# Masks of head pairs joined in one PSUM bank, and a retuned instruction order, in a two-layer hybrid attention decoder

## The chip, the cores and the metric

One core of a Trainium2 chip runs the whole program. Its engines are TensorE (PE, whose weight loads are listed as PEld), VectorE (DVE), ScalarE (ACT), GpSimd (POOL) and SyncE (SP), which issues the DMAs. The metric is the device time of one execution in microseconds (us), as the median of runs.

## The reference

Two layers on x of 512 tokens by 1024 channels. In a layer one normalised input goes through one input projection, whose columns are shared out among four groups of four heads of 64 channels each, and a gate. The outputs are normalised for each head, gated, projected and added to x. Cut to what the change touches:

```python
def fox_mixer(q, k, v, f_logit, fb):
    log_f = jax.nn.log_sigmoid(f_logit + fb)
    cum = jnp.cumsum(log_f, axis=1).transpose(0, 2, 1)
    for blk in range(T // Q_BLOCK):                       # 4 blocks of 128 queries
        s = q[:, :, t0:t1] @ k[:, :, :t1].T * ATTN_SCALE
        s = s + cum[:, :, t0:t1, None] - cum[:, :, None, :t1]
        mask = jnp.arange(t0, t1)[:, None] >= jnp.arange(t1)[None, :]
        p = _masked_softmax(s, mask)
        outs.append(p @ v[:, :, :t1])

def stick_breaking_mixer(q, k, v):
    for blk in range(T // Q_BLOCK):
        z = q[:, :, t0:t1] @ k[:, :, :t1].T * ATTN_SCALE
        mask = jnp.arange(t1)[None, :] < jnp.arange(t0, t1)[:, None]
        log_om = jnp.where(mask, jax.nn.log_sigmoid(-z), 0.0)
        suffix = lax.cumsum(log_om, axis=3, reverse=True) - log_om
        a = jnp.where(mask, jnp.exp(jax.nn.log_sigmoid(z) + suffix), 0.0)
        outs.append(a @ v[:, :, :t1])

for l in range(2):
    h = rmsnorm(x, norm_g[l])
    parts = split(h @ w_in[l])
    y = concat([hgrn2(...), fox_mixer(...), stick_breaking_mixer(...), nsa(...)])
    x = x + (headwise_rmsnorm(y) * out_norm_g[l] * silu(gate)) @ w_out[l]
return rmsnorm(x, final_norm_g)
```

HGRN2 is a gated linear recurrence in chunks of 64; NSA has a compressed, a selected and a window branch.

## The kernel before

The tokens lie in four blocks of 128. The input projection is done with split operands: the normalised and transposed x is held as a high part `hth` and a remainder `htl`, each weight as `whi` and `wlo`, and every product is three matmuls of 512 columns (hi by hi, hi by lo, lo by hi) for each of eight chunks, into PSUM tiles of the tag `pin`. ACT makes `whi`, DVE `wlo`, from the raw weights that SP's DMAs bring. PSUM has eight banks: four for `pin`, two for scores and for HGRN's small products (`pss`), one for attention outputs (`pso`), one for transposes of attention weights (`psm`).

FoX and stick-breaking go through the heads in pairs (i = 0, 1), through the four query blocks (`qb`, keys n = 128 to 512), and in a block through the two heads (s = 0, 1). A head's score takes a bank of `pss`: first a bf16 matmul of the identity with a 128x128 mask into the last 128 columns (in the trace `pss_pss<-one_c_bf`), then two score matmuls over all n columns. FoX then takes a negated maximum on DVE (`nm`) and an exponential on ACT with its row sum. Stick-breaking runs Abs, Exp, Ln on ACT, a DVE operation, a scan and a subtraction on DVE, and a last Exp on ACT, all on a tile `su` of the tag `t2`; the last of them that reads the scores is the subtraction. The function `turned` transposes the results with PE into the bank `psm` and copies them out as one tile `aT` (by `COPY`: DVE for FoX, ACT for the other two).

At the start each block of x is loaded (`XY`), its sum of squares is taken on ACT, `x_times_g` or `norm_t` multiplies it with the gain `gb` and the reciprocal root `xrs`, and PE transposes it. The multiply with the gain runs on POOL for the blocks in `POOLG`, else it is one DVE operation with the scaling:

```python
        if tb in POOLG:
            x_times_g(xg, gb, tb, 0, D, pool)
        norm_t(xg, xss, tb, None if tb in POOLG else gb)
```

The kernel isn't issued as it is written. All operations are recorded (so nearly all instructions have one line in the profile, that of the recorder), and `Program.order` then puts them in an order: it steps through a model of the five engines, and on each engine takes, of what could start, the operation with the lowest number in program order, shifted by `LEAD` (by tag) and `LAG` (projection matmuls go last). `RESERVE` keeps buffers of a tag back, `SLACK` stretches the model's costs and latencies, and `TIMES` sets when the pieces of each mixer come. `Program.issue` emits that order, and the engines follow their queues strictly. The figures in this model decide an order and nothing else.

Of the kernel before, what the change touches and what calls it, by code (L numbers as in the profile page):

```python
# [12 lines left out]
F32 = mybir.dt.float32  # L13
# [194 lines left out]
class Op:  # L208
    __slots__ = ("idx", "eng", "call", "reads", "writes", "cost", "deps", "new", "users", "wait", "prio", "lat",
                 "start", "done", "meth", "held", "pe", "form", "late")  # L210


class Program:
# [31 lines left out]
    def add(self, eng, call, writes, reads, cost, lat=0.0):  # L245
        o = Op()
        o.idx, o.eng, o.call, o.writes, o.reads, o.cost, o.lat = len(self.ops), eng, call, writes, reads, cost, lat
        o.prio, o.users, o.new, o.late = o.idx, [], [], False
# [24 lines left out]
        first = all(v.root.first is None for v in writes)  # L273
# [6 lines left out]
        o.late = eng == "pe" and first and writes[0].root.name in ("psf", "psb", "psq")  # L280
# [22 lines left out]
    def order(self):  # L303
# [34 lines left out]
        while n < len(ops):  # L338
            progress, nxt = False, math.inf
            for e in engines:  # L340
# [55 lines left out]
                elif e == "pe":  # L396
# [7 lines left out]
                    if o.late:  # L404

                        end = now + 0.08
                        begun = end
# [65 lines left out]
class Recorder:  # L473
# [28 lines left out]
    def cost(self, method, out, rest, kw, reads):  # L502
# [6 lines left out]
        elif self.name == "pe":  # L509
# [7 lines left out]
            load, stream, parts = m / 1.2, n / (2.227 if dt == F32R else 2.4), 1  # L517
# [36 lines left out]
def trunk(ctx: ExitStack, tc: tile.TileContext, cst, x, norm_g, w_in, lbl, fox_fb, pe_k, w1_k, w2_k,  # L554
# [234 lines left out]
    for l in range(nl):  # L789
# [387 lines left out]


        def fox(i):
            need(("fx", i))  # L1180
            Q1, Q2, K1, K2 = st["fx", i]
            for qb in range(NB):
# [32 lines left out]
        def stick(i):  # L1215
            need(("sb", i))
            Q1, K1, K2 = st["sb", i]
            for qb in range(NB):
# [3 lines left out]
                for s in range(2):  # L1222
                    ps = pss.tile([P, T], F32, name="psb", tag="pss")
                    pe.matmul(ps[:, qs], ident_b, mask_sb, start=True, stop=False, skip_group_check=True)
                    pe.matmul(ps[:, :n], Q1[:, s, qs], K1[:, s, :n], start=False, stop=False, skip_group_check=True)
                    pe.matmul(ps[:, :n], Q1[:, s, qs], K2[:, s, :n], start=False, stop=True, skip_group_check=True)
# [27 lines left out]
        def attend(qb):  # L1254
# [35 lines left out]
            for i in range(2):  # L1290
                us = {}
                for s in range(2):
                    for brs in ([slice(0, 2)] if qb < 2 else [slice(0, 1), slice(1, 2)]):
                        k = brs.stop - brs.start
                        ps = pss.tile([P, k, n], F32, name="psq", tag="pss")
                        pe.matmul(ps[:, :, qs], ident_b, mask_n.pattern([[0, k], [1, P]]), start=True, stop=False,
                                  skip_group_check=True)
# [153 lines left out]
TIMES = ((2.577, 1.29), (10.591, 0.535), (11.607, 0.725), (20.2, 0.497), (36.407, 0.974), (58.753, 0.361), (16.29, 1.112), (62.9, 0.953))  # L1451
RESERVE = {'gp_G': 1, 'pin_pin': 2, 'pso_pso': 3, 'sm_mr': 3, 't2_t2': 1, 'vp_vp': 3, 'psm_psm': 2}
# [39 lines left out]
```

## Time and profile before

| | |
|---|---|
| three runs | 672.25, 674.26, 674.77 us (median 674.26) |
| profiled execution, its own time | 672.69 us |
| its span | 670.9 us, mean granted clock 0.994 |
| PE busy | 655.9 us (98%), 5,387 matmuls |
| PEld busy | 515.1 us (77%) |
| DVE busy | 466.4 us (70%) |
| ACT busy | 419.0 us (62%) |
| POOL busy | 143.9 us (21%) |
| DMA moved | 63.68 MB, mean 95 GB/s |

The span runs from the first to the last instruction on the chip; the 1.8 us between it and the execution's time lie around it. Matmuls are pipelined, so the records of two of them overlap, and the distance of their starts tells what each takes of the engine. A time in brackets at the end of a row of the timeline is how long the engine stood idle before it, and the name behind it is what ended that.

### The profile page before, as it was taken

The page shows a single profiled execution, that of the slowest core. Times are in us where ns is not written, and L with a number is a line of the kernel's source. Part 1 is how long each engine was busy: PE and PEld are TensorE (multiplying, and loading weights), DVE is VectorE, ACT ScalarE, POOL GpSimd, SP SyncE. Part 2 cuts the span into 40 slices and gives each one's busy share as a digit, 9 for nine tenths or more (in the row PEclk, how much of TensorE's full clock was granted, in tenths as well). Part 3 has the DMA queues.
Part 4 walks back from the last instruction along what each step waited for, and adds up shares of the span by engine and source line. Part 5 has one row for each costly group of instructions (what it writes and reads, how often), then busy time and mean ns, then how long its engine had stood idle before and what let it go on. Part 6 is the DMA issues. An engine that isn't in the chain of part 4 may idle for free.

```text
span 670.9 us, 13843 instructions
## 1 busy us (share of the span) xinstructions
PE 655.9 (98%) x5387; PEld 515.1 (77%) x5387; DVE 466.4 (70%) x990; ACT 419.0 (62%) x942; POOL 143.9 (21%) x173
## 2 busy tenths in 40 slices
PE   7999999999999999999999999999999999999996
PEld 4788977778877777777888898777788777777774
DVE  4745588765878969754672476976678988786543
ACT  5455455666777879765353654566586778887632
POOL 3100223412333312210100030450223232122010
PEclk8999999999999999999999999999999999999998
DMA  6544243460433104112352425337124321420112
GB/s 235 164 105 113 67 136 98 113 156 1 127 94 97 48 32 143 64 64 94 104 161 59 106 64 144 83 95 190 33 71 133 90 63 41 127 79 5 44 64 94
DMA packets 67162, 63.68 MB, mean 95 GB/s; under 512 B 20484, under 2 KB 51736, under 8 KB 67096
## 3 DMA queue, kind: packets, MB, share of 16 engines
q1 hardware_dynamic: 67096, 62.80, 32.9%
q8 instruction: 42, 0.69, 0.4%
q14 instruction: 24, 0.20, 0.1%
HBM read 52.79 MB, written 4.19 MB: 85 GB/s over the span
## 4 chain that ended last, share of the span: by engine, by line
PE 93%; DVE 2%; issue 1%; DMA 1%; ACT 1%; SPq 1%; POOL 0%; POOLq 0%
PE pin_pin L490 64%; PE pss_pss L490 13%; PE pso_pso L490 9%; PE psm_psm L490 7%; DMA one_XY<-in_x 1%; SPq L490 1%; ACT t_t L490 0%; DMA sm_w<-in_nsa_cmp_w_v 0%; DVE wp_wlo L490 0%; ACT wp_whi L490 0%; POOL sm_rs L490 0%; DVE sm_vcm L490 0%; DVE one_htl L490 0%; DVE one_XY L490 0%; DVE sm_ng L490 0%
## 5 line engine op out<-in xcount | busy, mean ns | idle before, releaser
L490 PE MATMUL pin_pin<-wp_whi,one_hth 128*128 128x512 f32 (+1 forms) x384 | 152.7, 399 | 1.8 <-ACT wp_whi L490 1.8
L490 PE MATMUL pin_pin<-wp_wlo,one_hth 128*128 128x512 f32 (+1 forms) x384 | 152.8, 398 | 0.2 <-DVE wp_wlo L490 0.2
L490 PE MATMUL pin_pin<-wp_whi,one_htl 128*128 128x512 f32 (+1 forms) x384 | 150.1, 393 | 0.0
L490 DVE TENSOR_TENSOR wp_wlo<-wp_raw,wp_whi 128x1024 fp32r<-128x1024 f32 (+1 forms) x80 | 96.4, 1210 | 52.9 <-ACT wp_whi L490 52.2
L490 PE MATMUL pin_pin<-one_hth,wp_wlo 128*128 128x512 f32 x256 | 103.6, 405 | 0.0
L490 PE MATMUL pin_pin<-one_htl,wp_whi 128*128 128x512 f32 x256 | 103.0, 402 | 0.0
L490 PE MATMUL pin_pin<-one_hth,wp_whi 128*128 128x512 f32 x256 | 102.5, 401 | 0.0
L490 ACT ACTIVATE wp_whi<-wp_raw 128x1024 fp32r<-128x1024 f32 (+1 forms) x80 | 83.4, 1043 | 27.2 <-PE pin_pin L490 20.1
L490 POOL TENSOR_TENSOR sm_rs<-sm_ssv,one_mhalf 128x2 f32<-128x2 f32 (+1 forms) x48 | 41.4, 863 | 199.0 <-DVE sm_ssv L490 161.0
L490 PEld LDWEIGHTS pin_pin<-wp_whi,one_hth 128*128 128x128 f32 x384 | 72.4, 189 | 15.2 <-ACT wp_whi L490 2.0
L490 PEld LDWEIGHTS pin_pin<-wp_wlo,one_hth 128*128 128x128 f32 x384 | 72.6, 189 | 11.9 <-DVE wp_wlo L490 0.9
L490 PEld LDWEIGHTS pin_pin<-wp_whi,one_htl 128*128 128x128 f32 x384 | 72.5, 189 | 11.7
L490 ACT ACTIVATE t_t<-pss_pss,sm_nm 128x128 f32<-128x128 f32 (+3 forms) x96 | 50.9, 543 | 29.3 <-DVE sm_nm L490 25.6
L490 PE MATMUL pss_pss<-qk_qk,qk_qk 128*128 128x512 f32 (+3 forms) x224 | 66.8, 378 | 0.0
L490 DVE TENSOR_REDUCE sm_nm<-pss_pss 128x1 f32<-128x384 f32 (+5 forms) x80 | 43.2, 549 | 23.9 <-PE pss_pss L490 13.3
L490 PEld LDWEIGHTS pin_pin<-one_htl,wp_whi 128*128 128x128 f32 x256 | 48.3, 189 | 10.9 <-issue 0.4
L490 PEld LDWEIGHTS pin_pin<-one_hth,wp_wlo 128*128 128x128 f32 x256 | 48.3, 189 | 10.8 <-issue 0.7
L490 PE MATMUL psm_psm<-one_c_ident,t_t 128*128 128x128 f32 x320 | 55.6, 276 | 0.8 <-DVE sm_vcm L490 0.8
L490 PEld LDWEIGHTS pin_pin<-one_hth,wp_whi 128*128 128x128 f32 x256 | 48.2, 188 | 9.6 <-issue 0.4
L490 ACT ACTIVATE pa_pa<-pa_pa 128x512 f32<-128x512 f32 (+4 forms) x90 | 51.0, 568 | 6.8 <-DVE pa_pa L490 5.6
L490 POOL TENSOR_TENSOR h_h<-h_h,h_h 128x512 f32<-128x512 f32 (+1 forms) x16 | 26.5, 1658 | 118.4 <-ACT h_h L490 112.5
L490 PEld LDWEIGHTS psm_psm<-one_c_ident,t_t 128*128 128x128 f32 x320 | 39.7, 142 | 14.7 <-issue 3.2
(183 smaller groups left out, 1062.8 us busy)
## 6 DMA issues: line engine op xcount, KB each, us to landing
wp_raw<-in_w_in SPq DMA_DIRECT2D x56, 256.0 KB, 3.4
wp_raw<-in_w_in SPq DMA_DIRECT2D x28, 512.0 KB, 4.1
wp_raw<-in_w_out SPq DMA_DIRECT2D x16, 512.0 KB, 3.6
qk_qk<-qk_qk SPq DMA_DIRECT2D x16, 256.0 KB, 3.2
one_XY<-in_x SPq DMA_DIRECT2D x4, 512.0 KB, 7.7
pa_pa<-in_x SPq DMA_DIRECT2D x8, 256.0 KB, 3.2
xres<-one_XY SPq DMA_DIRECT2D x8, 256.0 KB, 2.0
pa_pa<-xres SPq DMA_DIRECT2D x8, 256.0 KB, 3.6
```

What stands on the lines that cost most here:

```text
L490: fn(*[r(a) for a in args], **{k: r(v) for k, v in kw.items()})
```

## The change

For the first two query blocks FoX and stick-breaking compute both heads of a pair in one bank: `heads_of(qb)` gives ((0, 1),) for qb below 2 and ((0,), (1,)) otherwise. One mask matmul covers both (`masked`, 2 x 128 columns). Stick-breaking runs each elementwise operation once over both heads, but for the scan, which stays one for each head, and has one `turned` for both. FoX takes the two maxima in one reduction; its exponentials stay one for each head. NSA's scores use the same helper and stay as they are.

In the model that sets the order, the load of bf16 weights costs m/4.8 in place of m/1.2, and the special case for the first matmul into a score bank (`late`) is gone. Several numbers of the tables change, `POOLG` and `LATEG` among them: block 2 in place of block 3 has its gain multiplied on POOL at the start, and at the boundary of the layers block 0 has its gain multiplied ahead of its root.

```diff
-        o.late = eng == "pe" and first and writes[0].root.name in ("psf", "psb", "psq")
...
-                    if o.late:
-
-                        end = now + 0.08
-                        begun = end
...
-            load, stream, parts = m / 1.2, n / (2.227 if dt == F32R else 2.4), 1
+            load, stream, parts = m / (4.8 if dt == BF else 1.2), n / (2.227 if dt == F32R else 2.4), 1
...
+        def heads_of(qb):
+
+            return ((0, 1),) if qb < 2 else ((0,), (1,))
+
+        def masked(name, mask, k, n, qs):
+
+            ps = pss.tile([P, k, n], F32, name=name, tag="pss")
+            pe.matmul(ps[:, :, qs], ident_b, mask.pattern([[0, k], [1, P]]), start=True, stop=False, skip_group_check=True)
+            return ps
...
-                for s in range(2):
-                    ps = pss.tile([P, T], F32, name="psf", tag="pss")
-                    pe.matmul(ps[:, qs], ident_b, mask_n, start=True, stop=False, skip_group_check=True)
-                    pe.matmul(ps[:, :n], Q1[:, s, qs], K1[:, s, :n], start=False, stop=False, skip_group_check=True)
-                    pe.matmul(ps[:, :n], Q2[:, s, qs], K2[:, s, :n], start=False, stop=True, skip_group_check=True)
-                    us += softmax(ps[:, None, :n], den[:, s:s + 1])
+                for hs in heads_of(qb):
+                    ps = masked("psf", mask_n, len(hs), n, qs)
+                    for j, s in enumerate(hs):
+                        pe.matmul(ps[:, j], Q1[:, s, qs], K1[:, s, :n], start=False, stop=False, skip_group_check=True)
+                        pe.matmul(ps[:, j], Q2[:, s, qs], K2[:, s, :n], start=False, stop=True, skip_group_check=True)
+                    us += softmax(ps, den[:, hs[0]:hs[-1] + 1])
...
-                    u = t2.tile([P, T], F32, name="su", tag="t2")[:, :n]
-                    act.activation(u, ps[:, :n], AF.Abs)
+                    u = t2.tile([P, k, n], F32, name="su", tag="t2")
+                    act.activation(u, ps, AF.Abs)
                     act.activation(u, u, AF.Exp, scale=-1.0)
                     act.activation(u, u, AF.Ln, bias=1.0)
-                    dve.scalar_tensor_tensor(u, ps[:, :n], 0.0, u, op0=OP.min, op1=OP.subtract)
-
-                    dve.tensor_tensor_scan(u.flip(), ones.to_broadcast([P, n]), u.flip(), 0.0, op0=OP.mult, op1=OP.add)
-                    dve.tensor_tensor(u, u, ps[:, :n], OP.subtract)
+                    dve.scalar_tensor_tensor(u, ps, 0.0, u, op0=OP.min, op1=OP.subtract)
+
+                    for j in range(k):
+                        dve.tensor_tensor_scan(u[:, j].flip(), ones.to_broadcast([P, n]), u[:, j].flip(), 0.0, op0=OP.mult, op1=OP.add)
+                    dve.tensor_tensor(u, u, ps, OP.subtract)
                     act.activation(u, u, AF.Exp)
-                    aT[s] = turned([u[:, kb * P:(kb + 1) * P] for kb in range(qb + 1)], COPY[1])
+                    t = turned([u[:, j, kb * P:(kb + 1) * P] for j in range(k) for kb in range(qb + 1)], COPY[1])
...
-POOLG = (3,)
-LATEG = (0, 1, 2, 3)
-SLACK = (1.15, 0.1, 1.0)
+POOLG = (2,)
+LATEG = (1, 2, 3)
+SLACK = (1.129, 0.119, 1.12)
```

Four of the eight pairs in `TIMES` change as well, `RESERVE` loses `pso_pso` and gains `wp_whi`, and `LEAD` changes for `qk_qk` (60 to 100) and `wp_wlo` (300 to 290).

PE's order at the first FoX block of the first layer, before (`one_c_bf` holds the bf16 identity and mask, `qk_qk` queries and keys, `pss_pss_0` and `pss_pss_1` are the two score banks):

```order
L490 MATMUL pin_pin_3_125<-one_hth_0_68,wp_wlo_0_99 128x512
L490 LDWEIGHTS one_c_bf_0_127
L490 MATMUL pss_pss_1_96<-one_c_bf_0_127 128x128
L490 MATMUL pss_pss_1_96<-qk_qk_1_137,qk_qk_0_136 128x128
L490 MATMUL pss_pss_1_96<-qk_qk_3_139,qk_qk_2_138 128x128
L490 LDWEIGHTS one_c_bf_0_127
L490 MATMUL pss_pss_0_95<-one_c_bf_0_127 128x128
L490 MATMUL pss_pss_0_95<-qk_qk_1_137,qk_qk_0_136 128x128
L490 MATMUL pss_pss_0_95<-qk_qk_3_139,qk_qk_2_138 128x128
L490 MATMUL pin_pin_3_125<-one_hth_0_68,wp_whi_0_104 128x512
```

The same place after the change:

```order
L484 MATMUL pin_pin_3_125<-one_hth_0_68,wp_wlo_0_99 128x512
L484 LDWEIGHTS one_c_bf_0_127
L484 MATMUL pss_pss_0_95<-one_c_bf_0_127 128x256
L484 MATMUL pss_pss_0_95<-qk_qk_1_137,qk_qk_0_136 128x128
L484 MATMUL pss_pss_0_95<-qk_qk_3_139,qk_qk_2_138 128x128
L484 MATMUL pss_pss_0_95<-qk_qk_1_137,qk_qk_0_136 128x128
L484 MATMUL pss_pss_0_95<-qk_qk_3_139,qk_qk_2_138 128x128
L484 MATMUL pin_pin_3_125<-one_hth_0_68,wp_whi_0_104 128x512
```

One mask of 256 columns stands where two of 128 stood, in one bank in place of two, and the four score matmuls follow it unchanged.

POOL's order at the start, before (`sm_xrs_0` to `sm_xrs_3` are the reciprocal roots of the four blocks, `one_XY` is x, `h4_h4_0` the gain; `h4_h4_3` and `h4_h4_4` are the normalised blocks 2 and 3):

```order
L490 TENSOR_TENSOR sm_xrs_0_91<-sm_xrs_0_91,one_mhalf_0_73 128x1
L490 TENSOR_TENSOR sm_xrs_1_92<-sm_xrs_1_92,one_mhalf_0_73 128x1
L490 TENSOR_TENSOR sm_xrs_2_93<-sm_xrs_2_93,one_mhalf_0_73 128x1
L490 TENSOR_TENSOR sm_xrs_3_94<-sm_xrs_3_94,one_mhalf_0_73 128x1
L490 TENSOR_TENSOR h4_h4_4_79<-one_XY_0_67,h4_h4_0_75 128x1024
```

and after:

```order
L484 TENSOR_TENSOR sm_xrs_0_91<-sm_xrs_0_91,one_mhalf_0_73 128x1
L484 TENSOR_TENSOR sm_xrs_1_92<-sm_xrs_1_92,one_mhalf_0_73 128x1
L484 TENSOR_TENSOR h4_h4_3_78<-one_XY_0_67,h4_h4_0_75 128x1024
L484 TENSOR_TENSOR sm_xrs_2_93<-sm_xrs_2_93,one_mhalf_0_73 128x1
L484 TENSOR_TENSOR sm_xrs_3_94<-sm_xrs_3_94,one_mhalf_0_73 128x1
```

POOL's large multiply moved from behind all four roots to between the second and the third, and is block 2's now. In the same place DVE multiplies block 3 with gain and root, and scales block 2 by its root alone.

DVE's order around the copies of the compressed values (`sm_vcm`, of which PE's next transposes need the bank `psm_psm_0`), before:

```order
L490 TENSOR_TENSOR pa_pa_0_110<-pa_pa_0_110,one_c_ropec_0_128 64x32
L490 COPY sm_vcm_0_172<-psm_psm_0_71 32x64
L490 TENSOR_TENSOR sm_kcs_0_170<-sm_kcs_0_170,pa_pa_0_110 64x32
L490 TENSOR_TENSOR one_XY_0_67<-pso_pso_0_156,sm_rs_1_164 128x128
L490 COPY sm_vcm_0_172<-psm_psm_0_71 32x64 x2
L490 SCALAR_TENSOR_TENSOR sm_ng_0_130<-sm_ng_0_130,pa_pa_4_114 128x48
L490 TENSOR_TENSOR sm_K1c_0_171<-sm_kcs_0_170,sm_K1c_0_171 64x32
L490 COPY sm_vcm_0_172<-psm_psm_0_71 32x64
```

and after:

```order
L484 STREAM_SHUFFLE pa_pa_0_110<-sm_kcr_0_169 64x32
L484 TENSOR_TENSOR pa_pa_0_110<-pa_pa_0_110,one_c_ropec_0_128 64x32
L484 TENSOR_TENSOR sm_kcs_0_170<-sm_kcs_0_170,pa_pa_0_110 64x32
L484 COPY sm_vcm_0_172<-psm_psm_0_71 32x64 x3
L484 TENSOR_TENSOR sm_K1c_0_171<-sm_kcs_0_170,sm_K1c_0_171 64x32
L484 COPY sm_vcm_0_172<-psm_psm_0_71 32x64
L484 SCALAR_TENSOR_TENSOR sm_ng_0_130<-sm_ng_0_130,pa_pa_4_114 128x48
```

Three of the four copies stand together now, a 64x32 subtraction stands ahead of the fourth, and the normalisation of `one_XY` and the operation on `sm_ng` have left the places between them. On PE, eight products into `pso_pso` (64x128) and one score of 384 columns stand now between the matmuls that these copies read and the next transposes, where eight projection matmuls stood.

## Rows read from the trace of the kernel before

**Rows 1.** Busy time of PE, PEld, DVE, ACT, POOL in one stretch, clock, DMA.

```profile
25.00:330.00 305.00, 302.94 (x2588) 239.23 (x2588) 214.03 (x466) 195.40 (x449) 67.07 (x79) 1.00 0.34 93
```

**Rows 2.** Waits of PE over the span: total us, times, longest.

```profile
PE pss_pss L490 <- issue: 3.0, 4, 1.3
...
PE psm_psm L490 <- DVE sm_vcm L490: 0.8, 2, 0.5
```

**Rows 3.** Timeline of PE, a 256-wide head under a 128-wide mask: start, duration.

```profile
132.74 0.23 PE L490 MATMUL pss_pss<-one_c_bf 128*128 128x128 bf16 x1
...
133.10 0.40 PE L490 MATMUL pin_pin<-wp_wlo,one_hth 128*128 128x512 f32 x1
```

**Rows 4.** Timeline of PE, 256-wide scores under a 256-wide mask.

```profile
244.44 0.28 PE L490 MATMUL pss_pss<-one_c_bf 128*128 128x256 bf16 x1
...
244.80 0.40 PE L490 MATMUL pin_pin<-wp_whi,one_hth 128*128 128x512 f32 x1
245.03 0.40 PE L490 MATMUL pin_pin<-wp_wlo,one_hth 128*128 128x512 f32 x1
```

**Rows 5.** Timeline of PE, two 128-wide heads next to each other.

```profile
112.12 0.23 PE L490 MATMUL pss_pss<-one_c_bf 128*128 128x128 bf16 x1
...
112.99 0.40 PE L490 MATMUL pin_pin<-one_htl,wp_whi 128*128 128x512 f32 x1
```

**Rows 6.** Timeline of PE, a 128-wide head by itself.

```profile
154.44 0.23 PE L490 MATMUL pss_pss<-one_c_bf 128*128 128x128 bf16 x1
...
155.02 0.78 PE L490 MATMUL pso_pso<-vp_vp,gp_G 128*128 128x64 f32 x6
```

**Rows 7.** Timeline of all engines in the opening norm.

```profile
11.73 2.44 DVE L490 TENSOR_TENSOR wp_wlo<-wp_raw,wp_whi 128x1024 fp32r<-128x1024 f32 x2
...
13.11 1.06 ACT L490 ACTIVATE t_t<-one_XY 128x1024 bf16<-128x1024 f32 x1 [0.20 <-DMA one_XY<-in_x]
...
15.24 0.40 PE L490 MATMUL pin_pin<-wp_wlo,one_hth 128*128 128x512 f32 x1
...
15.39 0.74 DVE L490 SCALAR_TENSOR_TENSOR h_h<-one_XY,sm_xrs,h_h 128x512 f32<-128x512 f32 x1
...
16.84 3.56 DVE L490 SCALAR_TENSOR_TENSOR h_h<-one_XY,sm_xrs,h_h 128x512 f32<-128x512 f32 x2 [0.59 <-POOL sm_xrs L490]
...
17.28 2.57 POOL L490 TENSOR_TENSOR h_h<-one_XY,h_h 128x1024 f32<-128x1024 f32 x1
...
17.35 0.60 PE L490 MATMUL pss_pss<-one_c_ident,h_h 128*128 128x128 f32 x4
...
19.30 0.60 PE L490 MATMUL pss_pss<-one_c_ident,h_h 128*128 128x128 f32 x4
...
21.06 0.66 PE L490 MATMUL pss_pss<-one_c_ident,h_h 128*128 128x128 f32 x4 [0.69 <-DVE one_htl L490]
...
22.85 0.50 PE L490 MATMUL pin_pin<-wp_wlo,one_hth 128*128 128x512 f32 x1 [0.22 <-DVE wp_wlo L490]
```

**Rows 8.** Page and PE's timeline: a burst, its wait, the instruction queue.

```profile
PE 655.9 (98%) x5387; PEld 515.1 (77%) x5387; DVE 466.4 (70%) x990; ACT 419.0 (62%) x942; POOL 143.9 (21%) x173
...
q8 instruction: 42, 0.69, 0.4%
...
114.83 1.21 PE L490 MATMUL pss_pss<-h_h 64*16 64x16 f32 x127
117.12 0.17 PE L490 MATMUL pss_pss<-h_h 64*16 64x16 f32 x1 [1.09 <-issue]
```

**Rows 9.** Timeline around the copies of compressed values.

```profile
219.08 0.23 DVE L490 COPY sm_vcm<-psm_psm 32x64 f32<-32x64 f32 x1
...
219.37 0.33 PE L490 MATMUL psm_psm<-one_c_ident,t_t 128*128 128x128 f32 x1 [0.52 <-DVE sm_vcm L490]
```

**Rows 10.** Groups on t_t: min, median, max ns, and forms.

```profile
L490 ACT ACTIVATE t_t<-t_t x96: 292/471/641, 161.6 to 569.3; 128x128 f32<-128x128 f32 x24, 128x256 f32<-128x256 f32 x24, 128x384 f32<-128x384 f32 x24, 128x512 f32<-128x512 f32 x24
...
L490 DVE TENSOR_TENSOR_SCAN t_t<-one_ones,t_t x32: 409/811/1224, 163.1 to 565.6; 128x128 f32<-128x128 f32 x8, 128x256 f32<-128x256 f32 x8, 128x384 f32<-128x384 f32 x8, 128x512 f32<-128x512 f32 x8
```

More of the change, by code (lines that the diff above doesn't have):

```diff
@@ L209 @@
     __slots__ = ("idx", "eng", "call", "reads", "writes", "cost", "deps", "new", "users", "wait", "prio", "lat",
-                 "start", "done", "meth", "held", "pe", "form", "late")
+                 "start", "done", "meth", "held", "pe", "form")
 class Program:
@@ L247, in add @@
         o.idx, o.eng, o.call, o.writes, o.reads, o.cost, o.lat = len(self.ops), eng, call, writes, reads, cost, lat
-        o.prio, o.users, o.new, o.late = o.idx, [], [], False
+        o.prio, o.users, o.new = o.idx, [], []
         if eng == "pe" and writes[0].root.tag.name == "pin_pin":
@@ L272, in add @@
                 r.acc = keep
-        first = all(v.root.first is None for v in writes)
         if eng == "pe":
@@ L1221, in stick @@
                 qs = slice(qb * P, n)
[L1222 to L1226, printed above, removed]
-                    u = t2.tile([P, T], F32, name="su", tag="t2")[:, :n]
-                    act.activation(u, ps[:, :n], AF.Abs)
+                for hs in heads_of(qb):
+                    k = len(hs)
+                    ps = masked("psb", mask_sb, k, n, qs)
+                    for j, s in enumerate(hs):
+                        pe.matmul(ps[:, j], Q1[:, s, qs], K1[:, s, :n], start=False, stop=False, skip_group_check=True)
+                        pe.matmul(ps[:, j], Q1[:, s, qs], K2[:, s, :n], start=False, stop=True, skip_group_check=True)
+                    u = t2.tile([P, k, n], F32, name="su", tag="t2")
+                    act.activation(u, ps, AF.Abs)
                     act.activation(u, u, AF.Exp, scale=-1.0)
                     act.activation(u, u, AF.Ln, bias=1.0)
-                    dve.scalar_tensor_tensor(u, ps[:, :n], 0.0, u, op0=OP.min, op1=OP.subtract)
-                    dve.tensor_tensor_scan(u.flip(), ones.to_broadcast([P, n]), u.flip(), 0.0, op0=OP.mult, op1=OP.add)
-                    dve.tensor_tensor(u, u, ps[:, :n], OP.subtract)
+                    dve.scalar_tensor_tensor(u, ps, 0.0, u, op0=OP.min, op1=OP.subtract)
+                    for j in range(k):
+                        dve.tensor_tensor_scan(u[:, j].flip(), ones.to_broadcast([P, n]), u[:, j].flip(), 0.0, op0=OP.mult, op1=OP.add)
+                    dve.tensor_tensor(u, u, ps, OP.subtract)
                     act.activation(u, u, AF.Exp)
-                    aT[s] = turned([u[:, kb * P:(kb + 1) * P] for kb in range(qb + 1)], COPY[1])
+                    t = turned([u[:, j, kb * P:(kb + 1) * P] for j in range(k) for kb in range(qb + 1)], COPY[1])
+                    for j, s in enumerate(hs):
+                        aT[s] = t[:, j * (qb + 1):(j + 1) * (qb + 1)]
                     yield
@@ L1294, in attend @@
                         k = brs.stop - brs.start
-                        ps = pss.tile([P, k, n], F32, name="psq", tag="pss")
-                        pe.matmul(ps[:, :, qs], ident_b, mask_n.pattern([[0, k], [1, P]]), start=True, stop=False,
-                                  skip_group_check=True)
+                        ps = masked("psq", mask_n, k, n, qs)
                         pe.matmul(ps, Q1[i][:, s, qs], K1[:, brs, :n], start=False, stop=False, skip_group_check=True)
@@ L1448, in trunk @@
     pr.issue(ctx, tc, order)
-TIMES = ((2.577, 1.29), (10.591, 0.535), (11.607, 0.725), (20.2, 0.497), (36.407, 0.974), (58.753, 0.361), (16.29, 1.112), (62.9, 0.953))
-RESERVE = {'gp_G': 1, 'pin_pin': 2, 'pso_pso': 3, 'sm_mr': 3, 't2_t2': 1, 'vp_vp': 3, 'psm_psm': 2}
+TIMES = ((2.577, 1.29), (10.591, 0.713), (11.607, 0.725), (20.2, 0.497), (50.852, 0.974), (58.753, 0.235), (13.999, 1.112), (62.9, 0.953))
+RESERVE = {'gp_G': 1, 'pin_pin': 2, 'sm_mr': 3, 't2_t2': 1, 'vp_vp': 3, 'psm_psm': 2, 'wp_whi': 2}
 FILL = (0, 1, 2, 6, 3, 4, 5, 7)
-LEAD = {'pin_pin': 20, 'psm_psm': -20, 'pss_pss': 10, 'qk_qk': 60, 'sm_mr': -80, 't2_k1': 120, 'vp_vp': -180, 'wp_wlo': 300, 'pa_junk': 0, 't2_t2': 0, 't2_oT': 40, 'gp_G': 10, 'pa_pa': 10, 'sm_nm': -10, 'one_htl': 100, 'one_hth': -20, 'wp_whi': 20}
+LEAD = {'pin_pin': 20, 'psm_psm': -20, 'pss_pss': 10, 'qk_qk': 100, 'sm_mr': -80, 't2_k1': 120, 'vp_vp': -180, 'wp_wlo': 290, 'pa_junk': 0, 't2_t2': 0, 't2_oT': 40, 'gp_G': 10, 'pa_pa': 10, 'sm_nm': -10, 'one_htl': 100, 'one_hth': -20, 'wp_whi': 20}
 FULL = (128, 128)
```

## The prediction

> **What bounds the kernel now.** The busy times by stretch come first [rows 1]: in the 305 us from 25 to 330 TensorE (PE) is busy for 302.94, VectorE (DVE) for 214.03, ScalarE (ACT) for 195.40, GpSimd (POOL) for 67.07, and the granted clock is full. So only two things can shorten the kernel: less work on PE, or fewer waits of PE. PE's waits were read next [rows 2]: the whole span has 3.0 us at "issue" (four times, waiting for nothing that the profile shows), and 0.8 us for the DVE copies into `vcm`; what else is listed lies in the first 25 us. Nearly all the rest is work. From there I went to PE's timeline, where the masks, the start and the two kinds of waits are priced. Work saved on ACT and DVE is worth nothing by itself; it counts only through what PE waits for. The last projection and the normalisation behind it keep their order, so I cost the tail at nothing.
>
> **What a removed mask is worth.** Sixteen of 32 masks of the first two query blocks go (2 layers x 2 pairs x 2 kinds of attention x 2 blocks = 16 joint blocks), and the 16 that stay are 256 columns wide. The 64 score matmuls of these blocks stay as they are. PE's records overlap, so I price by starts. A 256-wide head with a 128-wide mask occupies 132.74 to 133.10, 0.36 us [rows 3]. The same two score matmuls under a 256-wide mask, which the NSA scores have already, take 244.44 to 244.80, again 0.36 [rows 4]. So a mask twice as wide costs no more here; in this stream something other than its columns sets the pace.
>
> - Second query block (n = 256): now two heads at 0.36 are 0.72. Joint, it is 0.36 for mask and first head plus two 256-wide matmuls. A 512-wide matmul follows the one before it after 0.233 (244.80 to 245.03) [rows 4], and I take half of that for each, 2 x 0.117 = 0.23. Together 0.59, 0.13 saved, four times a layer.
> - First query block (n = 128): a lone head takes 154.44 to 155.02 with the projection matmul behind it, so 0.58 - 0.233 = 0.35 [rows 6]. Two adjacent heads take 112.12 to 112.99 less 0.233, 0.64, or 0.106 a matmul [rows 5]. Joint: 0.35 + 2 x 0.106 = 0.56. Three of four blocks of a layer have their heads apart in the order of before (0.70, saving 0.14), one has them adjacent (saving 0.08).
>
> A layer saves 4 x 0.13 + 3 x 0.14 + 0.08 = 1.02, both **2.0 us**. The bounds: 0 if the masks' columns were what PE is paced by (then nothing is removed, only rearranged), and 16 x 0.14 = 2.2 if all were apart.
>
> The Trainium skill, "TensorE: Matmul & The Clock Gate", section "Back-to-back issue gap", gives for the spacing of isolated warm matmuls the columns over 2.4 GHz plus 2.5 ns, and warns that short ones under-count this way. By that formula 16 masks of 256 columns instead of 32 of 128 would save an estimated 16 x 2.5 ns = 0.04 us: nothing. The two equal 0.36 us speak against it, and its own warning agrees with them.
>
> **The longer chains.** A joint block hands the transposes both heads at once, so the first head's comes later. For stick-breaking at n = 256 the chain is four passes of ACT, two of DVE and two scans. The longest passes, of 512 columns, take 0.641 on ACT [rows 10] and one of DVE's 0.74 (at 15.39) [rows 7]; a scan over 256 columns takes no more than the median of 0.811 [rows 10]: 4 x 0.64 + 2 x 0.74 + 2 x 0.81 = 5.7 us at work, perhaps 8 with the work that stands between in the queues (a factor I choose: DVE and ACT are busy two thirds of the time [rows 1]). What hides it is the distance in PE's order. Between the last score of such a block and its first transpose stand at least 37 matmuls of 512 columns, 37 x 0.233 = 8.6 us, beside 17 or more others; for n = 128, at least 25, 5.8 us, for a chain of some 4. The joint FoX blocks have at least 9, 2.1 us, for a maximum and two exponentials (about 1.2). So I take no wait. If the cover is gone, PE waits for the rest of the chain, and behind the transposes on PE's queue stands the projection that feeds everything else.
>
> **The start.** Here DVE waits for POOL. The two multiplies of DVE at 16.84 take 3.56 us, where a single one takes 0.74 at 15.39, and beside them POOL multiplies two SBUF operands from 17.28 for 2.57 [rows 7]. So DVE's second multiply stands still until POOL is done. PE then waits 0.69 at 21.06 and 0.22 at 22.85: 0.9 us. With POOL's multiply moved to block 2 and ahead of the reciprocal roots of blocks 2 and 3, it can begin when block 2 of x is in (ACT starts on it at 13.11) and DVE's pair of subtractions (11.73 to 14.17) ends. So I place it at 14.2 to 16.8. Then it holds up the multiply that ran at 15.39 until 16.8; that ends at 17.5, and PE's transposes of it stood at 17.35: up to 0.2 of wait. On POOL the roots of blocks 2 and 3 follow, so DVE's scaling of block 2 ends at perhaps 18.5, and PE wants that only at 19.30. Sum: -0.9 + 0.2 = -0.7, of which I take **-0.6**. Bounds: -0.9 if POOL hides entirely; and +0.6 if POOL gets its operands first and the second of the two subtractions waits for it, 2.57 late, to 16.7: PE needs that weight at 15.24, a wait of 1.5 in place of 0.9.
>
> The Trainium skill, "SBUF — State Buffer", section "Who interferes with whom", has this as a rule: POOL shares a port pair with DVE, a DVE instruction with two SBUF inputs is held by a POOL instruction that reads, and whoever issues first blocks the other for its whole length. The 3.56 us agree with it, and by it the bad bound is the likelier the earlier block 2 lands.
>
> **The waits at issue.** All four lie within bursts of tiny HGRN matmuls, as the 127 in 1.21 us with a wait of 1.09 behind them [rows 8]. PE's matmuls and weight loads are 5,387 each, 10,774 instructions, and the instruction queue moved 42 packets [rows 8], about 256 instructions each; 127 matmuls with their loads are 254, one packet. I read them as PE running out of fetched instructions when a burst uses up packets faster than they come. The change shifts where packets begin: 16 matmuls fewer and other neighbours of the bursts. By the new order's counts two of the four would shrink: **-0.5**, between -2 and +1.
>
> **The single bank of transposes.** PE waits 0.52 at 219.37 because its next transposes need the bank that the DVE copy of 219.08 empties, the fourth of four [rows 9]; 0.8 in both layers [rows 2]. In the new order only eight short products and one score stand between the matmuls and the next transposes, where 8 projection matmuls stood (8 x 0.233 = 1.9 us), and DVE still has a small subtraction ahead of the fourth copy. Against that, the copies come earlier in DVE's queue. Eight products and a score are about 0.9 us of cover, less by 1.0; the copies come perhaps 0.3 to 0.6 sooner. So the wait of 0.4 a layer grows to about 0.75: **+0.7** for both. Bounds -0.8 (none) and +2.5.
>
> The other retuned numbers move instructions elsewhere, where PE waits for nothing now; I cost them at nothing. The cover is the distance between an operand and its use on PE, and a row that lost it would cost one pass, up to 0.6 us.
>
> **Sum.** -2.0 - 0.6 - 0.5 + 0.7 = -2.4. The profiled execution took 672.69, so it would take 670.3. The three runs around it had 672.25, 674.26 and 674.77; the mean of all four is 673.5, and from there the median after is **671.1**.
>
> **Rivals.**
> - *The joint chains come late (slower).* Mechanism: PE reaches the transposes of the eight joint stick blocks before their last exponential is done. For it: 8 us in the queue against 8.6 of cover; against it: the projections are only a part of what stands between. It decides when the chain takes over 10 us in the queues. With 1.3 us of wait at each of eight blocks it is +10, and 672.69 - 2.4 + 10 + 0.8 = 681.
> - *Nothing is saved at the masks.* If the equal 0.36 were chance and columns were paid, only -0.6 - 0.5 + 0.7 = -0.4 is left: 673.1. By the skill's formula, above, the time would be this one too.
> - *New waits in the new order.* The bank of transposes at its upper bound (+2.5) and the start at its (+0.6): -2.0 + 2.5 + 0.6 = +1.1, 674.6.
> - *The waits vanish as well.* Masks -2.0, start -0.9, issue -2, bank -0.4: -5.3, 668.2.
>
> **Chances.** Forecast 0.52; better 0.22; nothing at the masks 0.10; new waits 0.08; late chains 0.08. This kernel's measurement can tell about 0.5%, 3.4 us, from no change: faster means under 670.9, slower over 677.6. My sum stands just at the lower edge, so faster has the better case and some of the forecast's own: 0.22 + 0.14 = 0.36; slower is late chains and a little of the new waits, 0.10; the rest, 0.54, is same. The range runs from the better case to the new waits, 668.0 to 674.6, which leaves out the late chains and the outer edges.
>
> **What would show it.** The table of PE's waits: no row of several us for psm on ACT (else the chains are late). The records of the masks: 16 fewer, and by starts 0.56 and 0.59 for a joint block. At 15 to 23 us: POOL's multiply ahead of 17, and no wait of PE at about 21. "Issue" at about 2.5 in the bursts; the wait for `vcm` near 1.5. I am wrong if PE's busy time falls by much less than 2 us with the waits unchanged, or if a new releaser stands at the head of the table.

## The result, and the profile after

The changed kernel takes 669.49 us (median of six runs, 668.66 to 670.69), the kernel before 672.84 (six runs, 672.25 to 674.77). The ratio of changed to before is 0.9944, with a 95% interval of [0.993, 0.9959]: 0.56% or some 3.8 us (3.4 by the medians), where 2.4 were forecast. Run once more beside other kernels it gave 0.9946 [0.9927, 0.9966]. The profiled execution took 669.13 us, 3.56 less than that of before.

The page of the changed kernel, its span and its busy times, which answer to the table of before:

```profile
span 667.3 us, 13759 instructions
...
PE 652.6 (98%) x5371; PEld 517.6 (78%) x5371; DVE 464.8 (70%) x968; ACT 415.5 (62%) x902; POOL 149.8 (22%) x173
...
q8 instruction: 42, 0.69, 0.4%
```

The span is 3.6 shorter and PE is busy 3.3 less, so in sum the gain is work or pace, and not waiting; single waits went and others came. The table of PE's waits (total, times, longest), against [rows 2]:

```profile
PE pso_pso L484 <- issue: 2.2, 1, 2.2
...
PE pin_pin L484 <- issue: 1.5, 1, 1.5
...
PE psm_psm L484 <- DVE sm_vcm L484: 0.9, 2, 0.5
PE pin_pin L484 <- DVE wp_wlo L484: 0.5, 1, 0.5
```

Issue went from 3.0 in four pieces to 3.7 in two, the wait for the copies into `vcm` from 0.8 to 0.9. Neither moved as I had said.

The joint block of the second query block on PE's timeline, against [rows 3]:

```profile
118.36 0.28 PE L484 MATMUL pss_pss<-one_c_bf 128*128 128x256 bf16 x1
118.40 0.71 PE L484 MATMUL pss_pss<-qk_qk,qk_qk 128*128 128x256 f32 x4
118.95 0.40 PE L484 MATMUL pin_pin<-one_htl,wp_whi 128*128 128x512 f32 x1
```

From 118.36 to 118.95 are 0.59 us, as worked out, where two lone heads took 2 x 0.36. A joint block of 128 columns takes 0.51 (108.71 to 109.22), where 0.56 was worked out. The table of waits has no row for the transposes of the joint blocks: the longer chains of ACT and DVE stayed covered.

The start, against [rows 7], on the timeline of POOL and DVE:

```profile
11.10 2.43 DVE L484 TENSOR_TENSOR wp_wlo<-wp_raw,wp_whi 128x1024 fp32r<-128x1024 f32 x2
...
12.48 3.31 POOL L484 TENSOR_TENSOR h_h<-one_XY,h_h 128x1024 f32<-128x1024 f32 x1 [2.35 <-DMA one_XY<-in_x]
...
14.71 1.63 DVE L484 SCALAR_TENSOR_TENSOR h_h<-one_XY,sm_xrs,h_h 128x512 f32<-128x512 f32 x1
```

POOL was issued while DVE's pair of subtractions ran and took 3.31 where it had taken 2.57; DVE then waited for it and took 1.63 in place of 0.74. That is the picture of the prediction, and the good one of its two bounds: DVE kept the operands, and PE lost nothing at 15 us. The waits at 21.06 and 22.85 are gone.

What the opening takes can be read by counting projection matmuls. The 49th starts at 28.49 before and at 27.15 after, with 55 other matmuls ahead of it in both. These rows count the projection matmuls (x48) up to just before that start; the granted clock stands third from the end:

```profile
0.00:28.48 28.48, 13.82 (x48) 0.94 0.64 216
0.00:27.14 27.14, 14.30 (x48) 0.94 0.70 225
```

From the first projection matmul (11.48 before, 10.85 after) to the 49th are 17.0 us before and 16.3 after: 0.7 less. From the 49th to the last (663.89 and 660.33) are 635.4 and 633.2: 2.2 less, although the waits in this stretch, at issue and for `vcm`, rose from 3.8 to 4.6.

### The profile page after: what moved, and what is told of

Same layout as the page of the kernel before. It is cut to its first block, busy times and chain, and to the rows that moved or that the text cites. A ratio compares the mean times of both kernels' runs of the same rounds, so it can differ in the third digit from the quotient of the medians.

```text
span 667.3 us, 13759 instructions
## 1 busy us (share of the span) xinstructions
PE 652.6 (98%) x5371; PEld 517.6 (78%) x5371; DVE 464.8 (70%) x968; ACT 415.5 (62%) x902; POOL 149.8 (22%) x173
## 4 chain that ended last, share of the span: by engine, by line
PE 95%; issue 2%; DVE 1%; DMA 1%; ACT 0%; SPq 0%; POOLq 0%; POOL 0%; DVEq 0%
PE pin_pin L484 67%; PE pss_pss L484 13%; PE pso_pso L484 9%; PE psm_psm L484 7%; DMA one_XY<-in_x 1%; DVE sm_vcm L484 0%; DVE sm_K1c L484 0%; SPq L484 0%; ACT t_t L484 0%; DVE wp_wlo L484 0%; DVE h_h L484 0%; ACT pa_pa L484 0%; ACT h_h L484 0%; DVE one_XY L484 0%; POOLq L1494 0%
## 5 line engine op out<-in xcount | busy, mean ns | idle before, releaser
L484 POOL TENSOR_TENSOR sm_rs<-sm_ssv,one_mhalf 128x2 f32<-128x2 f32 (+1 forms) x48 | 43.2, 901 | 204.6 <-DVE sm_ssv L484 200.6
L484 PE MATMUL pss_pss<-qk_qk,qk_qk 128*128 128x512 f32 (+3 forms) x224 | 65.1, 376 | 0.0
L484 DVE TENSOR_REDUCE sm_nm<-pss_pss 128x1 f32<-128x384 f32 (+3 forms) x72 | 42.8, 597 | 16.7 <-PE pss_pss L484 16.1
L484 PE MATMUL psm_psm<-one_c_ident,t_t 128*128 128x128 f32 x320 | 53.5, 275 | 0.9 <-DVE sm_vcm L484 0.9
L484 ACT ACTIVATE t_t<-psm_psm 128x512 f32<-128x512 f32 (+3 forms) x72 | 38.7, 538 | 18.0 <-PE psm_psm L484 17.6
```

The lines of the kernel that those rows point to most:

```text
L484: fn(*[r(a) for a in args], **{k: r(v) for k, v in kw.items()})
```

## The experiments

**One part of the change at a time.** Three kernels ask which part brings the gain: new tables and model with every head in a bank of its own, joint banks with the old tables and model, and joint banks with new tables and the old model.

```diff
 # separate: the changed kernel
-            return ((0, 1),) if qb < 2 else ((0,), (1,))
+            return ((0,), (1,))
 # joint_old: the kernel before, with fox, stick, heads_of and masked of the changed one
 # old_model: joint_old with TIMES, RESERVE, LEAD, POOLG, LATEG and SLACK of the changed one
```

> The changed kernel with every head in a bank of its own again, but with the new tables and the new model of weight loads. If the joint banks bring the gain (theory A: 16 masks fewer, 0.12 to 0.13 us each by PE's starts), 2.0 us come back: 669.5 + 2.0 = 671.5. If the new order of instructions brings it (theory B), the time stays at 669.5 within 1 us. The lone heads should read 0.36 (256 columns) and 0.35 (128 columns) again by starts.

> The kernel before with the joint banks alone: old tables, old model of weight loads. Theory A: 672.8 - 2.0 = 670.8, and a joint block of 256 columns reads 0.59 by starts. Theory B: 672.8 within 1 us. PE's waits at issue may move, since 16 matmuls fewer shift everything behind them; up to 1 us either way is put down to that.

> The changed kernel with the joint banks and the new tables, ordered by the old model of weight loads. Theory T (tables, model and list of operations fit each other, and any one alone gives an order with several us of new waits and more switches between projection and attention on PE): 675 or more, as the joint banks alone (678.8) and the new tables alone (684.4). Rival (the model of weight loads is a detail): 669.5 within 1.5 us.

Measured: separate 684.42 (1.0158 [1.0136, 1.018]), joint_old 678.81 (1.0075 [1.0052, 1.0098]), old_model 676.58 (1.0048 [1.0032, 1.0065]). Theories A and B both missed, and by far: each part without the others is slower than the kernel before. Theory T, which was made after the first two results, held for the third. Its new waits are there (in the run with the old model PE waits 2.7 for `vcm` and 2.1 for ACT at the transposes). That the order switches more often between projection and attention isn't shown: the run with the old model leaves the projection 234 times behind its opening, the changed kernel 242 times. PE's waits in the kernel with separate heads:

```profile
PE pin_pin L484 <- issue: 4.1, 2, 2.3
PE psm_psm L484 <- ACT t_t L484: 2.6, 6, 0.9
...
PE pso_pso L484 <- DVE one_XY L484: 1.4, 4, 0.4
```

It has waits at transposes and products that neither of the two kernels has, and PE is busy 663.1 us with the same matmuls as before (655.9). The 320 transposes of attention weights take 38.6 us to the next start, added up, against 28.8 before; 2.3 of this is one of the waits at issue, and some stand where their input is late. The clock takes a part too: in this execution the granted clock is 0.91 from 110 to 130 us and from 440 to 460, where it was full in the two profiled executions above, and 0.09 of 40 us is some 3.6 us of work (an estimate). How the rest divides stays open. What these three runs settle is the method: an edit to what is recorded changes the whole order, so parts of this change can be priced only where the order is held.

**The price of a mask, order held.** In the changed kernel's own order, the 256-column masks are issued as two of 128, first one right behind the other (all 32 of them, NSA's too), then, for FoX and stick-breaking alone, the second just ahead of the second head's scores.

```diff
 # narrow_masks: in masked(), order as recorded
+                    for j in range(k):
+                        nc.tensor.matmul(ps[:, j, qs].real(), ident_b.real(), mask.real(), start=(j == 0), ...)
 # mask_per_head: j = 0 there, j = 1 issued ahead of the first matmul of head 1
```

> The changed kernel in its own order, with each of the 32 masks of 256 columns (16 of FoX and stick-breaking, 16 of NSA) issued as two of 128 columns one behind the other; the scores are the same. If a mask has a price by the instruction, of 0.12 us (theory A), this costs 32 x 0.12 = 3.8 us, 673.3, and a joint block reads 0.71 by starts in place of 0.59. If the second mask costs only the 0.04 by which a score matmul starts behind its mask, 1.3 us, 670.8. If columns are paid (rival), nothing: 669.5.

> The changed kernel in its own order, with the joint masks of FoX and stick-breaking cut into two of 128 columns, the second of them just ahead of the second head's scores; all else is joint. By PE's starts of the run with narrow masks the instruction itself costs 0.05 to 0.07 us; what a head of its own cost beyond that is the wait of the first score matmul behind its mask (0.20 in place of 0.12 us at 256 columns, 0.14 in place of 0.11 at 128). Theory A2 (the gain of the joint bank is one mask and one such wait a block): a block of 256 columns reads 0.71 in place of 0.59, one of 128 columns 0.06 to 0.08 more, in all 8 x 0.12 + 8 x 0.07 = 1.5 us, 1.002 of the changed kernel. Rival (the mask alone): 16 x 0.06 = 1.0 us. Rival (the joint elementwise work brings it): nothing.

Narrow masks: 673.82 (1.0008 [0.9991, 1.0025]), 4.3 above the changed kernel. The timeline of PE at a joint block of 256 columns:

```profile
203.04 0.29 PE L1183 MATMUL pss_pss<-one_c_bf 128*128 128x128 bf16 x2
203.13 0.72 PE L484 MATMUL pss_pss<-qk_qk,qk_qk 128*128 128x256 f32 x4
203.69 0.40 PE L484 MATMUL pin_pin<-one_hth,wp_whi 128*128 128x512 f32 x1
```

0.65 in place of 0.59. So a mask more is worth 0.06 us at the same number of columns, half of theory A's 0.12 and not nothing; 32 of them are 2 us. The rest of the 4.3 isn't the masks' own: in the profiled execution the waits at issue have grown to 4.7, and the granted clock is 0.91 from 110 to 130 us and 0.83 from 440 to 460.

Mask by head: 674.31 (1.0014 [0.9993, 1.0034]). The same block:

```profile
202.78 0.24 PE L1182 MATMUL pss_pss<-one_c_bf 128*128 128x128 bf16 x1
202.83 0.48 PE L484 MATMUL pss_pss<-qk_qk,qk_qk 128*128 128x256 f32 x2
203.15 0.23 PE L1182 MATMUL pss_pss<-one_c_bf 128*128 128x128 bf16 x1
203.19 0.48 PE L484 MATMUL pss_pss<-qk_qk,qk_qk 128*128 128x256 f32 x2
203.51 0.40 PE L484 MATMUL pin_pin<-one_hth,wp_whi 128*128 128x512 f32 x1
```

0.73, a little over the 0.71 of theory A2: the second half of a head's price is that its first score starts the next one only 0.20 behind, where later scores follow at 0.12. But the time rose by 4.7 where 1.5 was expected. The waits at issue had grown to 4.2, and behind one of them the clock fell. Busy times by stretch, granted clock third from the end:

```profile
438.00:441.00 3.00, 0.80 (x93) 0.70 (x83) 3.00 (x5) 2.56 (x7) 1.33 (x2) 0.88 0.20 68
441.00:443.00 2.00, 1.98 (x8) 1.81 (x9) 2.00 (x3) 1.61 (x5) 1.88 (x4) 0.50 0.90 253
443.00:445.00 2.00, 2.00 (x6) 1.32 (x4) 1.93 (x5) 1.31 (x3) 1.82 (x4) 0.50 0.48 107
445.00:447.00 2.00, 2.00 (x8) 1.29 (x7) 0.05 (x1) 0.00 (x0) 1.80 (x5) 0.50 0.19 41
```

From about 440.4 to 447 PE has half its clock, 1.2 GHz. This made the next questions: what these waits are, and whether the masks' price can be had without them.

**The waits at issue.** Two kernels test whether PE runs out of fetched instructions. One moves 12 projection matmuls ahead of the sixth burst of small HGRN matmuls in each layer; the other adds 64 tiny matmuls in the opening. The changed kernel runs beside them.

The code is shortened.

```diff
 # spread12: order = pr.order(), then for the sixth burst of each layer
+        order, n = pull(ops, order, order.index(i), 12)   # the next 12 projection matmuls go ahead of it
 # shift64: behind the last warm-up matmul
+                for _ in range(64):
+                    nc.tensor.matmul(pz[:16, :16].real(), zero[:, :16].real(), zero[:, :16].real(), start=True, stop=True)
```

> The changed kernel once more, as the measure for the three that run beside it. 0.994 of the kernel before; PE's waits at issue 2.2 and 1.5 us at about 113 and 438 us; the start of the first projection matmul anywhere between 10.8 and 11.5 us if that is the landing of the first DMAs.

> The changed kernel with 12 projection matmuls (2.8 us) moved ahead of the sixth burst of small HGRN matmuls in each layer, and nothing else moved. If PE waits at issue because the bursts use up fetched instructions faster than they come (theory F), the 2.2 and 1.5 us behind these bursts go and nothing takes their place: 669.5 - 3.7 = 665.8. If the wait is tied to the burst itself (rival), it stays, behind the burst, 2.8 us later: 669.5.

> The changed kernel with 64 matmuls of 16 columns more (and their weight loads, 128 instructions) in the opening, where PE waits for the first weights; the order behind them is the same. If instructions come in packets of about 256 (theory F), every packet begins half a packet elsewhere, and the two waits at issue change in size or place by 0.5 us or more. If the bursts alone set them (rival), they read 2.2 and 1.5 us again. The start costs up to 1 us.

After again: 669.63 (0.9946 [0.9927, 0.9966]); the waits at issue read 2.2 and 1.4, the first projection matmul started at 10.96 (before 11.48, after 10.85).

Spread: 669.45 (0.993 [0.9905, 0.9954]). The first waits of its table:

```profile
PE pss_pss L484 <- ACT t_k L484: 2.9, 4, 0.8
...
PE psm_psm L484 <- DVE sm_vcm L484: 0.9, 2, 0.5
```

There is no wait at issue left: theory F, and the rival is out. But the matmuls that were moved had covered the next scores, which now wait for ACT to empty the burst's banks, in all 2.9; and behind these waits the granted clock is 0.62 from 118 to 122 us in this execution, some 1.5 us of work by estimate. The 665.8 was missed for that.

Shift: 670.95 (0.9988 [0.9962, 1.0014]). The waits stand at other bursts than in the changed kernel, in the middle of them, here two of three on its timeline:

```profile
101.06 0.27 PE L484 MATMUL pss_pss<-h_h 64*32 64x32 f32 x8 [1.45 <-issue]
...
429.12 0.25 PE L484 MATMUL pss_pss<-h_h 64*32 64x32 f32 x4 [1.67 <-issue]
```

The order there is the same and only the count of instructions ahead has changed by 128, so place and size go by the count, as theory F has it.

The transfers of instructions themselves are in the traces. In the changed kernel the instruction queue moves nothing from 108.9 to 113.2 us, and from 113.2 to 116.2 one packet, beside the wait from 113.83 to 116.05:

```profile
q8 instruction: 1, 0.02, 2.3%
```

By the trace's DMA records this packet of 16 KB starts at 113.50 and has landed at 114.59, and PE goes on 1.46 us later. All 22 waits at issue of over 1 us in the layers, over the traces of all runs, have one such packet, which has landed 1.2 to 1.7 us before the wait ends. So that PE waits for instructions is shown, and not only argued.

**The terms at the start and at the boundary.**

```diff
 # pool_block3
-POOLG = (2,)
+POOLG = (3,)
 # lateg_all
-LATEG = (1, 2, 3)
+LATEG = (0, 1, 2, 3)
```

> The changed kernel with POOL's large multiply given back to block 3. If moving it brought 0.6 us, this gives 670.1, with a DVE multiply of over 2.5 us and a wait of PE of some 0.7 us at about 20 to 21 us. If the 0.6 us by which the changed kernel's first projection matmul started earlier (10.85 against 11.48) was only the landing of the first DMAs in that execution, the time stays at 669.5, and the start of the first projection matmul varies over these four runs by as much.

> The changed kernel with the gain of block 0 multiplied late again at the boundary of the layers. PE never waits there in either kernel, so nothing: 669.5, 0.994 to 0.996 of the kernel before. If the boundary held a part of the gain that the masks don't explain (1 to 1.5 us at equal clock), it comes back here: 670.7.

Pool at block 3: 669.08 (0.9941 [0.992, 0.9961]), the same as the changed kernel, although its profile has the old picture again:

```profile
16.30 3.54 DVE L484 SCALAR_TENSOR_TENSOR h_h<-one_XY,sm_xrs,h_h 128x512 f32<-128x512 f32 x2 [0.59 <-POOL sm_xrs L484]
...
16.73 2.56 POOL L484 TENSOR_TENSOR h_h<-one_XY,h_h 128x1024 f32<-128x1024 f32 x1
...
20.50 0.66 PE L484 MATMUL pss_pss<-one_c_ident,h_h 128*128 128x128 f32 x4 [1.36 <-DVE one_htl L484]
```

The wait is there. In the whole time its price can't be told: the two intervals together allow a difference of some 1.7 us either way. The profiled execution itself, 672.78, is the slowest of the seven, for another reason: its granted clock is 0.83 from 110 to 130 us, which is some 3.4 us of work (an estimate).

In the opening the price can be read. At equal clock the run to compare with is the covered kernel of below, which opens in the changed kernel's order: in both the granted clock was full from 13 to 16 us, and the first projection matmul started at 10.97 here and at 11.00 there. The 49th starts at 27.93 here and at 26.43 there:

```profile
0.00:27.92 27.92, 12.91 (x48) 1.00 0.69 220
0.00:26.42 26.42, 12.94 (x48) 1.00 0.70 229
```

So POOL's multiply at block 3 costs 1.5 us of the opening at full clock. With POOL at block 3 the stretch from the first to the 49th takes 17.0 us at each clock that was met from 13 to 16 us (1.00 here, 0.72 before, 0.61 in the run with joint banks and old tables). With POOL at block 2 it takes 15.4 at 1.00, 16.3 at the changed kernel's 0.61 (there PE ran at half speed for some 2.3 of the 3 us, worth 1.2 us of work) and 16.5 at 0.51. At half clock PE asks later for what DVE delivers, and less of DVE's delay shows; so the move brings 0.5 to 1.5 us, by the clock of the execution. Late gain: 669.07 (0.9936 [0.9914, 0.9958]), nothing, as expected.

**The waits covered.** The last two kernels put the first together: 11 projection matmuls ahead of the sixth burst, taken from behind the next joint scores so that those keep their cover, and four ahead of the transposes that wait for `vcm`; then the same with the masks by head. The code is in outline.

```diff
 # covered
+        past = last score matmul of the next joint block behind the burst
+        order = pull(ops, order, order.index(pe[b]), 11, order.index(past))   # from behind `past`
+        ...
+        order = pull(ops, order, order.index(pe[k]), 4, order.index(pe[k]))   # pe[k]: first transpose behind pv_
 # covered_per_head: covered, with the masks of mask_per_head
```

> The changed kernel with 11 projection matmuls moved ahead of the sixth HGRN burst of each layer, taken this time from behind the next joint scores, so that these keep the cover that the run with 12 moved matmuls took from them; and 4 moved ahead of the transposes that wait for the copies of compressed values. If theory F holds and the wait for t_k in the run before was only lost cover, the waits at issue (3.6), for t_k (2.9) and for the copies (0.9) are all gone, the clock has no reason to fall behind them, and the time is 669.5 - 3.6 - 0.9 = 665.0. If the bursts only push their waits onto whatever comes next (rival), it stays at the 669 of that run.

> The kernel with the covered bursts, and in it the joint masks of FoX and stick-breaking cut in two again, the second ahead of the second head's scores. Without waits at issue to disturb it this is the price of 16 masks alone. Theory A2 (a mask and the wait of the first score behind it): 8 x 0.12 + 8 x 0.07 = 1.5, up to 2.0 by the sums of the prediction: 664.3 + 1.5 to 2.0 = 665.8 to 666.3. Rival (only the instruction): 16 x 0.06 = 1.0, 665.3. If the 4.6 us of the run with the masks cut in the changed kernel were the masks' own price: 668.9.

Covered: 664.29 us (four runs, 663.63 to 664.60), 0.986 [0.9836, 0.9883] of the kernel before: it beats both kernels, with the same instructions as the changed one in another order. PE's waits in the whole span:

```profile
PE pin_pin L484 <- ACT wp_whi L484: 1.4, 1, 1.4
PE psm_psm L484 <- DVE one_ones L484: 1.0, 1, 1.0
PE pin_pin L484 <- DVE wp_wlo L484: 0.5, 1, 0.5
PE pss_pss L484 <- issue: 0.3, 1, 0.3
PE pss_pss L484 <- DVE sm_xrs L484: 0.3, 1, 0.3
```

Masks by head in it: 665.85 (0.9891 [0.9874, 0.9909]), 1.6 us more by medians and 2.1 by the ratios, about what theory A2 and the prediction's sums gave (1.5 to 2.0); but the two intervals overlap, so these times don't part it from the rival's 1.0. The traces do better, since the order is the same. The clock of the opening differs (1.00 in the one, 0.50 in the other from 13 to 16 us) and puts the 49th projection matmul 0.8 later; from there to the last one are 629.1 us in the covered kernel and 630.1 with masks by head:

```profile
0.00:27.24 27.24, 14.48 (x48) 0.94 0.69 225
...
655.54 0.39 PE L484 MATMUL pin_pin<-wp_whi,one_htl 128*128 128x512 f32 x1
...
657.39 0.39 PE L484 MATMUL pin_pin<-wp_whi,one_htl 128*128 128x512 f32 x1
```

The first and the last row are of the run with masks by head. That is 1.0 more, with the last wait at issue of 0.3 gone: the masks' own price is 1.3, between the rival's 1.0 and theory A2's 1.5.

## Why the prediction was right, and where its steps were not

**The masks: the mechanism was right, the size a little high.** Forecast -2.0. With the order held and the long waits gone, undoing them costs 1.3 us by the traces, 1.6 to 2.1 by the run times; a joint block reads the 0.59 of the sum. What I had as the price of one instruction is two things, 0.06 for the mask and the rest for the first score behind it; the sum did not depend on which, since it was taken from whole heads. The Trainium skill, "TensorE: Matmul & The Clock Gate", section "Back-to-back issue gap", by its formula for isolated matmuls would have given an estimated 0.04 us for all sixteen; the runs decide against the formula, and for the section's warning that it under-counts short ones.

**The longer chains: right.** No wait at a joint block's transposes in the changed kernel; the slow rival, 681, did not come.

**The start: right.** -0.6 was forecast, and -0.7 is read in the profiled pair from the first projection matmul to the 49th. POOL and DVE did what was said. What the prediction didn't have is that the size goes by the clock of the execution: 1.5 at full clock. The first projection matmul is 0.63 earlier besides (10.85 against 11.48). Other runs with the same opening have 10.73 to 11.54, so this is the scatter of single executions, and no gain.

**The waits at issue: the cause was right, the sign wrong.** -0.5 was forecast, +0.7 measured by the table of waits (3.0 to 3.7). The step that failed is "by the new order's counts two of the four would shrink": they did go, and the other two grew. The bounds, -2 to +1, held it.

**The single bank: wrong in size.** +0.7 was forecast, +0.1 measured (0.8 to 0.9). Two steps failed. "Less by 1.0": PE was ready for the transposes 1.8 us after the matmuls that the copies read (214.99 to 216.82 in the changed kernel), against 2.5 before (216.37 to 218.85), so the cover fell by 0.65. The eight products are sixteen matmuls on the timeline and take 1.0 us, with 0.4 for the score, where 0.9 was put for both. And "the copies come perhaps 0.3 to 0.6 sooner": the fourth starts 2.0 behind those matmuls (216.99), against 2.7 (219.08 [rows 9]), 0.7 sooner. The two cancel.

**The sum.** -2.0 - 0.6 - 0.5 + 0.7 would read, with the measured terms, -1.3 to -2.1 for the masks, -0.7, +0.7 and +0.1: -1.2 to -2.0. The profiled pair has -3.6, or -2.9 without the 0.63 of scatter, and the run times -3.4 to -3.8. So 1 to 2 us of the gain come from what I had at nothing, "The other retuned numbers". In the profiled pair this lies behind the opening: there PE's work fell by 3.0 (2.2 of time and 0.8 of added waits), at full clock in both, and the masks are worth 1.3 to 2.1 of it. Which places hold the rest stays open: no single wait went that is as large. The boundary of the layers brought nothing that its run can tell. The three kernels that lack the tables, the model or the joint banks are 7 to 15 us slower than the changed one; that shows that the parts need each other, and not how the gain is shared out among them.

That the forecast was 1 us or so short and still held is in part the width of its range: 668.0 to 674.6 takes in no change at all. By its own marks the median of 669.49 counts as faster (under 670.9), to which it gave 0.36, against 0.54 for same.

**The basis.** I took the scatter of before (672 to 675) as noise and added 0.8 for it. For the changed kernel a cause shows: the same wait at issue leaves the clock alone in one execution and not in the next. Two executions of the changed kernel by stretch, each with 2.2 us of wait at about 114; the one of the result:

```profile
112.00:114.00 2.00, 1.83 (x131) 1.77 (x132) 2.00 (x5) 1.85 (x4) 0.00 (x0) 1.00 0.55 203
114.00:116.00 2.00, 0.00 (x0) 0.00 (x0) 2.00 (x4) 1.85 (x8) 1.83 (x2) 1.00 0.13 17
116.00:118.00 2.00, 1.95 (x11) 1.50 (x11) 1.97 (x4) 1.38 (x5) 1.83 (x4) 1.00 0.89 251
118.00:120.00 2.00, 2.00 (x13) 1.54 (x12) 1.51 (x4) 0.83 (x1) 1.82 (x4) 1.00 0.59 137
```

and the one that ran beside the experiments:

```profile
114.00:116.00 2.00, 0.16 (x2) 0.13 (x2) 2.00 (x3) 1.88 (x7) 1.51 (x2) 0.87 0.06 12
116.00:118.00 2.00, 1.63 (x5) 1.38 (x5) 2.00 (x3) 1.44 (x5) 1.88 (x3) 0.50 0.99 259
118.00:120.00 2.00, 2.00 (x7) 1.34 (x6) 1.81 (x4) 1.06 (x1) 1.82 (x4) 0.50 0.59 133
120.00:122.00 2.00, 2.00 (x8) 1.48 (x8) 0.00 (x0) 0.00 (x0) 1.80 (x5) 0.50 0.01 2
```

At 0.50 PE started 7 or 8 matmuls in 2 us in place of 11 to 13. The 381st projection matmul starts at 110.44 and 110.77 in these two, the 441st at 133.01 and 136.04: 2.7 of the 2.8 us between the two executions arise there. For the kernel before there is no trace of a slower execution; that its 672.60 has a mean clock of 0.999 and its 676.67 one of 0.990 fits the same cause and doesn't show it. Cutting 16 masks in two cost 4.7 us in the changed kernel and 1.6 in the covered one: with the long waits gone, the clock of the covered kernel stays full in the layers, and its four runs lie within 1 us.

## What to carry to other kernels

An engine that is 98% busy can still hide one per cent in a handful of waits: read the table of waits for "issue", see what runs just ahead of it, and move independent work in between from a place that doesn't need it as cover. Where a scheduler derives the order from numbers, an edit and its retuning are one change; price a part of it by holding the order and altering only what is issued at each place. And compare executions by their granted clock before a difference of half a per cent is explained.

## What the runs showed of the hardware

- PE waits of 1.1 to 2.7 us for nothing but instructions, behind or within bursts of 128 matmuls of 16 or 32 columns (1.2 to 1.3 us a burst). In the changed kernel the bursts at 106.46 and 111.93 are 5.5 us apart, with 2.2 us of wait behind the second; with 2.8 us more of projection between them no such wait is left, with 2.6 us one of 0.3. 128 instructions more in the opening move the waits to other bursts. At each wait of over 1 us a packet of instructions has landed 1.2 to 1.7 us before PE goes on.
- A bf16 mask ahead of fp32r scores of 256 columns costs 0.06 us for itself, and the first score then holds back the second to 0.20 us where later ones follow at 0.12.
- The clock went to 0.50 behind some of those waits, once for some 6.5 us (440.4 to 447, with PE idle from 438.8 to 441.0), and stayed at 1.00 behind the same wait in another execution.
- A DVE multiply of 0.74 us took 1.63 beside a POOL multiply on SBUF operands, and a pair of them 3.54 to 3.56. On PE this cost 1.5 us of the opening at full clock and 0.5 to 0.7 where the clock was at half for most of the 3 us before.
